# Strassen's scheme in one decoder layer: thirteen early weight sums built by adding transfers in DRAM instead of on VectorE

## Chip, cores, metric

One core of one Trainium2 chip runs the whole kernel in one launch. The metric is the device time in microseconds (us); lower is better. Names of the engines: TensorE (PE) multiplies matrices, VectorE (DVE) and ScalarE (ACT) work element by element, GpSimd (POOL) does little work of its own here and issues transfers on a software queue (q0 in the profile), SyncE (SP) issues the weight loads on a hardware queue (q1). All transfers are moved by the same 16 DMA engines.

## The reference, cut to what matters

One layer of a decoder trunk over 256 tokens of width 2048, all in float32:

```python
a = rmsnorm(h, attn_norm)
proj = a @ w_in                        # 2048 x 5184: MLA q, latent, rope key, MoBA q, k, v
kv = rmsnorm(c_kv, kv_norm) @ w_ukv    # 512 x 2048
...
h = h + concat(out_mla, out_moba) @ w_o            # 2048 x 2048
f = rmsnorm(h, ffn_norm)
h = h + (silu(f @ w_gate) * (f @ w_up)) @ w_down   # 2048 x 5632, twice, and back
g = sigmoid(rmsnorm(h, ple_norm) @ w_ple_gate)     # 2048 x 2048
h = h + g * (p @ w_ple_proj)
return rmsnorm(h, final_norm)
```

## The kernel before, in words

**Products in three parts.** Every float32 operand is split into a high part (rounded to float32r) and a low part (the rest), and a product is three matmuls that accumulate in one bank of PSUM: high x high, low x high, high x low (`three`, L385 to L390). For a weight tile, ACT makes the high part by a cast (`split_hi`, L337), and DVE the low part by a subtraction (`split_lo`, L348). The parts go into a ring of 12 places of 512 columns (`ringh`, `ringl`), later also into `more` and `most`.

**Units and groups.** The work is a list of units; a unit is a pair of 128-row tiles of a weight matrix with up to 1024 columns, 1 MB, loaded by SP (`load`, L220) into one of three buffers (`raw`; five from the MLP on). A group is all units of one output: ga, q0, u0, q1, u1, qk0, qk1, v (the attention's projections), wo0 and wo1 (its output), then g0, g1 and so on for gate and u0, u1 and so on for up of the MLP, d for down, and pg, pe at the end. The columns of q1 (512) and the two halves of qk0 and qk1 (512 each) are loaded in rows of 2 KB, most others in rows of 4 KB. A buffer is free again when both splits of its unit are done. The load of unit i+3 stands in the program at unit i; SP issues it as soon as the buffer is free. Inside ACT and DVE all work is in the order of the program, and attention, norms and the emptying of banks are woven in between the splits by a list of tasks (`add`, `step`).

**The start.** x arrives already turned; ACT and DVE split it (`x_parts`) and form the sum of its squares. When ga's last product is done, ACT takes the square root that x's norm needs (L157), DVE finishes the norm's factor, and ACT empties ga's banks (L860) so that q0's products may start.

**Strassen's scheme.** In the MLP (from its second group on; the MLP's up groups carry the names u0 to u4 as well) most units use the scheme with seven products instead of eight: for a weight block with quarters b11, b12, b21, b22, the products use b11, b22, b21 and four sums of quarters t1 to t4 on the weights' side, and four sums S1 to S4 of quarters of the activations (made in `act_transpose` at L140 to L143, and in `sums_of`). `seven` issues the seven products and, at a group's end, combines them (L465 to L469). The weight sums of an ordinary unit are made by DVE in place in its buffer (L347, L350, L351).

**Early sums.** For 13 of these units (`EARLY`: three of g1, two each of u1, u2, u3, u4, one each of g2 and g3) the sums are made long before, while attention runs. The task `early_sums` (L356 to L376) does it unit by unit: POOL loads the block from DRAM into the SBUF tile `wsums` (L366), the task waits until PE has been given a certain number of columns, DVE makes the sums by three subtractions (L372 to L374), and POOL stores the four sums, 128 x 2048, into a DRAM tile (L376). When the unit's turn comes in the MLP, SP loads b11, b21, b22 from the weights (L209, L210) and the four sums from that tile (L211). The tiles `wsums` stand in SBUF places that later hold other things (`f0l`, `more_sums`). The task starts at unit 5 of ga, on two units first, and with the rest at unit 8; a copy of one element on POOL (L364) makes the first transfer wait for the load that is three units ahead.

**Adding transfers.** POOL can issue a transfer that adds to its target. Before the change the kernel does so in the MLP: `gate_add` (`stage<-U`, L1018), `add_later` (`hd<-copied`, L937, its target in DRAM) and `split_hi` of some units of down (`morel<-raw`, L336). POOL issues in the order of the program; an instruction that waits holds up all behind it.

Of the kernel before, what the change touches and what calls it, by code (L numbers as in the profile page):

```python
# [8 lines left out]
F32 = mybir.dt.float32  # L9
# [4 lines left out]
ALU = mybir.AluOpType  # L14
# [21 lines left out]
def kernel(ctx, tc, x, w_in, w_ukv, w_o, w_gate, w_up, w_down, w_ple_gate, w_ple_proj,  # L36
                             final_norm, x_turned, p_turned, columns_in, out):
    nc = tc.nc
# [73 lines left out]
    def act_transpose(src, k0, g0, dst, kd0=None, scaled=False, sums=None):  # L112

        kd0 = k0 if kd0 is None else kd0
        part = src[:, :, k0 * 128:k0 * 128 + 256]
        if scaled:
            part = S["nrm"][:, (k0 // 2) % 2]
        b = obank()  # L120
        for i in range(2):
            for t in range(NT):
                nc.tensor.transpose(b[:, (2 * i + t) * 128:(2 * i + t + 1) * 128],  # L123
                                    part[:, t, i * 128:(i + 1) * 128], ident)
        if sums is None:
            both = [(dst[0][:, kd0 + i, :], dst[1][:, kd0 + i, :], b[:, i * 256:(i + 1) * 256],
                     gain[:, g0 + k0 + i:g0 + k0 + i + 1]) for i in range(2)]
            for hi, _, ps, g in both:
                nc.scalar.mul(hi, ps, g)
            for hi, lo, ps, g in both:  # L130
                nc.vector.scalar_tensor_tensor(lo, ps, g, hi.bitcast(F32), op0=ALU.mult, op1=ALU.subtract)
            return
        whole, some = S["nrm"][:, 2], S["nrm"][:, 3]
        for i in range(2):
            nc.scalar.mul(whole[:, i], b[:, i * 256:(i + 1) * 256], gain[:, g0 + k0 + i:g0 + k0 + i + 1])
        split_psum(dst[0][:, kd0:kd0 + 2, :], dst[1][:, kd0:kd0 + 2, :], whole)
        a11, a21, a12, a22 = (whole[:, i, t * 128:(t + 1) * 128] for i in range(2) for t in range(2))
        four = some.rearrange("q a (b c) -> q (a b) c", b=2)
        tt = nc.vector.tensor_tensor
        tt(four[:, 0], a21, a22, op=ALU.add)  # L140
        tt(four[:, 2], a21, a11, op=ALU.subtract)
        tt(four[:, 1], four[:, 0], a11, op=ALU.subtract)
        tt(four[:, 3], a12, four[:, 1], op=ALU.subtract)  # L143
        split_psum(sums[0], sums[1], four)

    def square_sum(src, acc):
# [192 lines left out]
    def split_lo(jb, c0=0, c1=None, n=1, row=slice(None)):  # L339

        if units[jb.unit].adding:
            return
        h, l, r = (x[:, row] for x in by_row_tile(n, *parts_of(jb), raw_of(jb)))
        tt = nc.vector.tensor_tensor
        f = quarters(jb) if jb.kind == "21" and not units[jb.unit].early else None
        if f is not None:
            tt(f[:, 0:2], f[:, 1:2].to_broadcast([128, 2, 512]), f[:, 0:4:3], op=ALU.subtract)  # L347
        tt(l[:, :, c0:c1], r[:, :, c0:c1], h[:, :, c0:c1].bitcast(F32), op=ALU.subtract)  # L348
        if f is not None:
            tt(f[:, 3], f[:, 3], f[:, 0], op=ALU.subtract)  # L350
            tt(f[:, 2], f[:, 2], f[:, 3], op=ALU.subtract)  # L351

    todo_early = []

    def early_sums(tag, enough, wait, landed=None):

        made = 0
        while todo_early and made < enough:
            u = todo_early.pop(0)
            made += 1  # L360
            f = big.tile([128, 4, 512], F32, name="wsums", tag=tag)
            (w, c0, _), k0 = u.srcs[0], u.ks[0] * 128
            if landed is not None:
                nc.gpsimd.tensor_copy(f[:, 0, 0:1], landed)  # L364
                landed = None
            nc.gpsimd.dma_start(f.rearrange("q (k a) c -> q k (a c)", k=2),  # L366
                                w[k0:k0 + 256, c0:c0 + 1024].rearrange("(k q) c -> q k c", q=128))
            since = columns[0]
            while columns[0] < since + wait() or S["crowded"]:
                yield 1  # L370
            tt = nc.vector.tensor_tensor
            tt(f[:, 0:2], f[:, 1:2].to_broadcast([128, 2, 512]), f[:, 0:4:3], op=ALU.subtract)  # L372
            tt(f[:, 3], f[:, 3], f[:, 0], op=ALU.subtract)
            tt(f[:, 2], f[:, 2], f[:, 3], op=ALU.subtract)  # L374
            u.early = dram.tile([128, 2048], F32, name=f"wsums{u.name}{u.idx}")
            nc.gpsimd.dma_start(u.early, f.rearrange("q a c -> q (a c)"))  # L376

    def split(jb):
        if not jb.cast:
# [62 lines left out]
    def seven(u, turn):  # L442
# [18 lines left out]
        if turn == 3 and u.sevens_end:  # L461
            U = S["U"] = big.tile([128, NT, 1024], F32, name="U", tag="vb")
            c1, c2 = U[:, :, 0:512], U[:, :, 512:1024]
            tt = nc.vector.tensor_tensor
            nc.scalar.copy(c1[:, 0], st["m1"])  # L465
            tt(c2[:, 0], c1[:, 0], st["m6"], op=ALU.add)
            tt(c1[:, 1], c2[:, 0], st["m7"], op=ALU.add)
            tt(c2[:, 0], c2[:, 0], st["m5"], op=ALU.add)
            tt(c2[:, 1], c1[:, 1], st["m5"], op=ALU.add)  # L469
            B["rot"], B["next"] = st["free"], 0  # L470
            if u.into is not None:
                def join(hs=S["h"][:, :, u.into:u.into + 1024]):
                    tt(hs, hs, U, op=ALU.add)
                    yield 1
                add(join())

    def sums_of(parts, k0, pairs, at, tag="vb"):

        for n, kk in enumerate(pairs):
            both = big.tile([128, 2, 2, SEQ], F32, name="both", tag=tag)  # L480
            whole, some = both[:, 0], both[:, 1]
            h, l = (x[:, kk - k0:kk - k0 + 2] for x in parts)
            tt = nc.vector.tensor_tensor
            tt(whole, h.bitcast(F32), l.bitcast(F32), op=ALU.add)
            a11, a21, a12, a22 = (whole[:, i, t * 128:(t + 1) * 128] for i in range(2) for t in range(2))
            hi, lo = (aT[i][:, at + 2 * n:at + 2 * n + 2] for i in range(2))
            four = some.rearrange("q a (b c) -> q (a b) c", b=2)
            tt(four[:, 0], a21, a22, op=ALU.add)
            tt(four[:, 1], four[:, 0], a11, op=ALU.subtract)
            tt(four[:, 2], a21, a11, op=ALU.subtract)  # L490
            tt(four[:, 3], a12, four[:, 1], op=ALU.subtract)
            split_psum(hi, lo, some)
            yield 1

# [834 lines left out]
    for i, u in enumerate(units):  # L1329
# [5 lines left out]
        S["long"] = u.name in ("ga", "q0", "u0", "wo0", "wo1")  # L1335
        S["crowded"] = u.name == "v" and u.idx > 0 or u.name == "wo0" and u.idx < 4
        if u.name == "ga" and u.idx == 5:
            todo_early.extend(x for x in units if x.early)
            add(early_sums("f0l", 2, lambda: 53248, raw[i + 3][:, 0, 0:1]))
        if u.name == "ga" and u.idx == 8:  # L1340
            add(early_sums("more_sums", 99, lambda: 57344 if S["long"] else 34816))
        if u.name == "g1" and u.idx == 0:
            S["mid"] = S.pop("turned")
        if u.name == "wo0":
# [87 lines left out]
```

## Time and profile before

| what | value |
|---|---|
| median of 3 runs | 1180.9 us (1180.17 to 1181.25) |
| the profiled execution | 1180.28 us, of which the span of the program is 1178.5 us |
| idle share of PE by the page | 1% |
| matmuls | 5477 |
| bytes moved by DMA | 287.80 MB, mean 244 GB/s |
| loads of wsums by POOL | 13 of 1 MB, issued from 31.7 to 326.2 us |
| stores of wsums by POOL | 13 of 1 MB, issued from 57.7 to 343.7 us |

In the page's slices (40 of 29.5 us), PE is full in all but the last, and the granted PE clock is at nine tenths or more throughout. The DMA row is highest at the start:

```profile
PE   9999999999999999999999999999999999999996
PEld 7888888899888888888888888888888888888886
DVE  6866756776557689999999899989998989897474
ACT  6745746456456756667566666757575756465453
DMA  9896787755683776686959596868868795846531
```

Each digit is the busy share of a slice in tenths. DVE is at 5 to 8 tenths over attention (the first 14 slices) and near full in the MLP.

### The profile page before, as it was taken

What the parts mean: (1) busy time and instruction counts of PE and PEld (TensorE: products, weight loads), DVE (VectorE), ACT (ScalarE), POOL (GpSimd) and SP (SyncE); (2) the same over time, 40 slices, a digit from 0 to 9 for tenths busy, and PEclk for the clock granted to TensorE, in tenths of its full rate; (3) what the DMA queues carried; (4) which work ended last, traced back from release to release, by engine and by line L of the source; (5) the groups of instructions that cost most, each with busy time, mean ns of one, the idle gap of its engine ahead of it and who ended that gap; (6) DMA issues with size and microseconds to landing.
All of it is one profiled execution on the core that took longest, in us unless ns stands there. A gap on an engine that the chain in (4) does not pass through costs nothing.

```text
span 1178.5 us, 14590 instructions
## 1 busy us (share of the span) xinstructions
PE 1167.4 (99%) x5477; PEld 978.3 (83%) x5477; DVE 952.9 (81%) x1127; ACT 710.7 (60%) x898; POOL 50.2 (4%) x73
## 2 busy tenths in 40 slices
PE   9999999999999999999999999999999999999996
PEld 7888888899888888888888888888888888888886
DVE  6866756776557689999999899989998989897474
ACT  6745746456456756667566666757575756465453
POOL 5000000000000000000000000000000000000000
PEclk9999999999999999999999999999999999999999
DMA  9896787755683776686959596868868795846531
GB/s 328 298 337 202 288 299 258 267 185 206 220 330 130 280 260 220 235 283 208 353 171 334 154 348 210 291 214 321 240 214 255 283 276 195 326 153 218 201 107 72
DMA packets 85880, 287.80 MB, mean 244 GB/s; under 512 B 5681, under 2 KB 7985, under 8 KB 81201
## 3 DMA queue, kind: packets, MB, share of 16 engines
q1 hardware_dynamic: 76352, 239.71, 56.7%
q0 software_dynamic: 8880, 46.14, 14.2%
q10 hardware_dynamic: 576, 1.02, 0.3%
q8 instruction: 43, 0.70, 0.2%
q14 instruction: 29, 0.23, 0.1%
HBM read 252.24 MB, written 26.21 MB: 236 GB/s over the span
## 4 chain that ended last, share of the span: by engine, by line
PE 95%; DMA 2%; ACT 1%; DVE 1%; SPq 0%; issue 0%; ACTq 0%; DVEq 0%
PE bank L390 30%; PE bank L388 30%; PE bank L389 30%; DMA raw<-in_w_in 2%; PE bank L591 1%; PE bank L1052 1%; PE bank L123 1%; PE bank L620 1%; ACT ringh L337 1%; PE bank L614 0%; PE bank L594 0%; PE bank L726 0%; DMA xT<-in_x_turned 0%; PE bank L621 0%; ACT aT L109 0%
## 5 line engine op out<-in xcount | busy, mean ns | idle before, releaser
L337 ACT CAST ringh<-raw 128x1024 fp32r<-128x1024 f32 (+5 forms) x310 | 372.7, 1239 | 274.9 <-PE bank L389 112.0
L348 DVE TENSOR_TENSOR ringl<-raw,ringh 128x1024 fp32r<-128x1024 f32 (+5 forms) x310 | 444.7, 1457 | 101.9 <-ACT ringh L337 100.0
L388 PE MATMUL bank<-ringh,aT 128*128 128x512 f32 (+3 forms) x713 | 274.7, 385 | 0.2
L390 PE MATMUL bank<-ringl,aT 128*128 128x512 f32 (+3 forms) x713 | 270.8, 380 | 0.0
L389 PE MATMUL bank<-ringh,aT 128*128 128x512 f32 (+3 forms) x713 | 270.3, 379 | 0.0
L390 PEld LDWEIGHTS bank<-ringl,aT 128*128 128x128 f32 x713 | 134.1, 188 | 25.3 <-DVE ringl L348 0.9
L388 PEld LDWEIGHTS bank<-ringh,aT 128*128 128x128 f32 x713 | 134.2, 188 | 24.7 <-ACT ringh L337 1.0
L389 PEld LDWEIGHTS bank<-ringh,aT 128*128 128x128 f32 x713 | 134.3, 188 | 23.8 <-DVE aT L658 0.2
L337 ACT CAST moreh<-raw 128x1024 fp32r<-128x1024 f32 (+2 forms) x70 | 79.8, 1173 | 19.9 <-DVE raw L347 9.2
L348 DVE TENSOR_TENSOR morel<-raw,moreh 128x1024 fp32r<-128x1024 f32 (+2 forms) x66 | 85.5, 1317 | 1.8 <-ACT moreh L337 1.3
L388 PE MATMUL bank<-ringh,ffTh 128*128 128x512 f32 x204 | 79.5, 390 | 0.0
L337 ACT CAST most<-raw 128x1024 fp32r<-128x1024 f32 (+2 forms) x58 | 56.8, 1005 | 37.5 <-DVE raw L347 14.4
L390 PE MATMUL bank<-ringl,ffTh 128*128 128x512 f32 x204 | 79.4, 389 | 0.0
L389 PE MATMUL bank<-ringh,ffTl 128*128 128x512 f32 x204 | 79.4, 389 | 0.0
L348 DVE TENSOR_TENSOR most<-raw,most 128x1024 fp32r<-128x1024 f32 (+2 forms) x58 | 66.3, 1164 | 1.6 <-ACT most L337 1.5
L347 DVE TENSOR_TENSOR raw<-raw 128x1024 f32<-128x1024 f32 x51 | 62.5, 1225 | 1.7
L389 PEld LDWEIGHTS bank<-ringh,ffTl 128*128 128x128 f32 x204 | 38.3, 188 | 8.0
L388 PEld LDWEIGHTS bank<-ringh,ffTh 128*128 128x128 f32 x204 | 38.3, 188 | 7.9
L390 PEld LDWEIGHTS bank<-ringl,ffTh 128*128 128x128 f32 x204 | 38.3, 188 | 7.9
L351 DVE TENSOR_TENSOR raw<-raw 128x512 f32<-128x512 f32 x51 | 35.3, 692 | 1.8
L350 DVE TENSOR_TENSOR raw<-raw 128x512 f32<-128x512 f32 x51 | 34.9, 684 | 0.0
L388 PE MATMUL bank<-most,aT 128*128 128x512 f32 x88 | 34.6, 394 | 0.0
(356 smaller groups left out, 1958.6 us busy)
## 6 DMA issues: line engine op xcount, KB each, us to landing
raw<-in_w_down SPq DMA_DIRECT2D x44, 1024.0 KB, 7.2
raw<-in_w_gate SPq DMA_DIRECT2D x35, 1024.0 KB, 7.4
raw<-in_w_up SPq DMA_DIRECT2D x32, 1024.0 KB, 7.5
raw<-in_w_in SPq DMA_DIRECT2D x40, 512.0 KB, 5.4
raw<-in_w_o SPq DMA_DIRECT2D x16, 1024.0 KB, 5.6
raw<-in_w_ple_gate SPq DMA_DIRECT2D x16, 1024.0 KB, 5.0
raw<-in_w_in SPq DMA_DIRECT2D x8, 1024.0 KB, 5.0
wsums<-in_w_up POOLq DMA_DIRECT2D x8, 1024.0 KB, 7.1
```

The source lines that it names most:

```text
L123: nc.tensor.transpose(b[:, (2 * i + t) * 128:(2 * i + t + 1) * 128], part[:, t, i * 128:(i + 1) * 128], ident)
L337: nc.scalar.copy(h[:, :, c0:c1], r[:, :, c0:c1])
L347: tt(f[:, 0:2], f[:, 1:2].to_broadcast([128, 2, 512]), f[:, 0:4:3], op=ALU.subtract)
L348: tt(l[:, :, c0:c1], r[:, :, c0:c1], h[:, :, c0:c1].bitcast(F32), op=ALU.subtract)
L350: tt(f[:, 3], f[:, 3], f[:, 0], op=ALU.subtract)
L351: tt(f[:, 2], f[:, 2], f[:, 3], op=ALU.subtract)
L388: nc.tensor.matmul(b, xh, h, start=start, stop=False)
L389: nc.tensor.matmul(b, xl, h, start=False, stop=False)
L390: nc.tensor.matmul(b, xh, l, start=False, stop=stop)
L591: nc.tensor.matmul(s[:, c0:c0 + nk], qT[:, q * 128:(q + 1) * 128], kT[:, 0:nk], start=True, stop=qpe is None)
L620: nc.tensor.matmul(o[:, 0:256], v(0), pT[:, 0:256], start=True, stop=False)
L1052: nc.tensor.transpose(b[:, (2 * i + t) * 128:(2 * i + t + 1) * 128], st[:, t, (k + i) * 128:(k + i + 1) * 128], ident)
```

## The change

The early sums no longer pass through SBUF and DVE. For each of the 13 units, POOL copies quarters of the weight block straight into the unit's DRAM tile and then lets transfers add to it, in four rounds: b11 into the first and the fourth place, b22 into the second, b21 into the third; then b12 is added to the first and second; then the second is added to the fourth; then the fourth to the third. Two units are taken together, round by round. All of these transfers are issued at unit 5 of ga, as one list on POOL, with no waiting for columns; what orders them is only their dependence on each other. A transfer of a round waits for the landing of those of the round before.

So that additions suffice, the signs of the scheme are turned: t1 to t4 of the ordinary units and S1 to S4 are formed with other signs and operands, in the same number of instructions of the same shapes, and two combinations at a group's end become `m5 - c2` and `m5 - c1`.

```diff
         tt = nc.vector.tensor_tensor
-        tt(four[:, 0], a21, a22, op=ALU.add)
-        tt(four[:, 2], a21, a11, op=ALU.subtract)
+        tt(four[:, 0], a21, a22, op=ALU.subtract)
+        tt(four[:, 2], a11, a21, op=ALU.subtract)
         tt(four[:, 1], four[:, 0], a11, op=ALU.subtract)
-        tt(four[:, 3], a12, four[:, 1], op=ALU.subtract)
+        tt(four[:, 3], four[:, 1], a12, op=ALU.add)
...
         if f is not None:
-            tt(f[:, 0:2], f[:, 1:2].to_broadcast([128, 2, 512]), f[:, 0:4:3], op=ALU.subtract)
+            tt(f[:, 0:2], f[:, 1:2].to_broadcast([128, 2, 512]), f[:, 0:4:3], op=ALU.add)
...
-            tt(f[:, 3], f[:, 3], f[:, 0], op=ALU.subtract)
-            tt(f[:, 2], f[:, 2], f[:, 3], op=ALU.subtract)
+            tt(f[:, 3], f[:, 3], f[:, 0], op=ALU.add)
+            tt(f[:, 2], f[:, 2], f[:, 3], op=ALU.add)
...
-    def early_sums(tag, enough, wait, landed=None):
...
-            f = big.tile([128, 4, 512], F32, name="wsums", tag=tag)
...
-            nc.gpsimd.dma_start(f.rearrange("q (k a) c -> q k (a c)", k=2),
-                                w[k0:k0 + 256, c0:c0 + 1024].rearrange("(k q) c -> q k c", q=128))
-            since = columns[0]
-            while columns[0] < since + wait() or S["crowded"]:
-                yield 1
-            tt = nc.vector.tensor_tensor
-            tt(f[:, 0:2], f[:, 1:2].to_broadcast([128, 2, 512]), f[:, 0:4:3], op=ALU.subtract)
-            tt(f[:, 3], f[:, 3], f[:, 0], op=ALU.subtract)
-            tt(f[:, 2], f[:, 2], f[:, 3], op=ALU.subtract)
-            u.early = dram.tile([128, 2048], F32, name=f"wsums{u.name}{u.idx}")
-            nc.gpsimd.dma_start(u.early, f.rearrange("q a c -> q (a c)"))
+    def early_sums(them, landed):
+
+        nc.gpsimd.tensor_copy(const.tile([128, 1], F32, name="landed"), landed)
+
+        def sums_of_one(u):
+            u.early = dram.tile([128, 2048], F32, name=f"wsums{u.name}{u.idx}")
+            e = u.early.rearrange("q (a c) -> q a c", a=4)
             (w, c0, _), k0 = u.srcs[0], u.ks[0] * 128
+            b11, b12, b21, b22 = (w[k0 + 128 * k:k0 + 128 * k + 128, c0 + c:c0 + c + 512].rearrange(
+                "q (a c) -> q a c", a=1) for k in range(2) for c in (0, 512))
+            nc.gpsimd.dma_start(e[:, 0:4:3], b11.to_broadcast([128, 2, 512]))
+            nc.gpsimd.dma_start(e[:, 1:2], b22)
+            nc.gpsimd.dma_start(e[:, 2:3], b21)
+            yield
+            nc.gpsimd.dma_start(e[:, 0:2], b12.to_broadcast([128, 2, 512]), accum_op=ALU.add)
+            yield
+            nc.gpsimd.dma_start(e[:, 3:4], e[:, 1:2], accum_op=ALU.add)
+            yield
+            nc.gpsimd.dma_start(e[:, 2:3], e[:, 3:4], accum_op=ALU.add)
+
+        for n in range(0, len(them), 2):
+            both = [sums_of_one(u) for u in them[n:n + 2]]
+            while both:
+                both = [g for g in both if next(g, g) is None]
...
-            tt(c2[:, 0], c2[:, 0], st["m5"], op=ALU.add)
-            tt(c2[:, 1], c1[:, 1], st["m5"], op=ALU.add)
+            tt(c2[:, 0], st["m5"], c2[:, 0], op=ALU.subtract)
+            tt(c2[:, 1], st["m5"], c1[:, 1], op=ALU.subtract)
...
         if u.name == "ga" and u.idx == 5:
-            todo_early.extend(x for x in units if x.early)
-            add(early_sums("f0l", 2, lambda: 53248, raw[i + 3][:, 0, 0:1]))
-        if u.name == "ga" and u.idx == 8:
-            add(early_sums("more_sums", 99, lambda: 57344 if S["long"] else 34816))
+            early_sums([x for x in units if x.early], raw[i + 3][:, 0, 0:1])
```

On POOL, behind the rotary tables in ga, this stood before the change (out<-in, a load of `wsums` is L366, a store L376):

```order
L364 COPY wsums<-raw_114 128x1
L366 DMA wsums<-in_w_gate 128x2x1024 x2
L376 DMA wsumsg_535<-wsums 128x2048
L366 DMA wsums<-in_w_gate 128x2x1024
L376 DMA wsumsg_654<-wsums 128x2048
L366 DMA wsums<-in_w_up 128x2x1024
```

And this stands there now; `wsumsg_326` and `wsumsg_330` are the DRAM tiles of the first two units, L363 to L365 the copies, L367, L369 and L371 the three rounds of adding:

```order
L363 DMA wsumsg_326<-in_w_gate 128x2x512
L364 DMA wsumsg_326<-in_w_gate 128x512
L365 DMA wsumsg_326<-in_w_gate 128x512
L363 DMA wsumsg_330<-in_w_gate 128x2x512
L364 DMA wsumsg_330<-in_w_gate 128x512
L365 DMA wsumsg_330<-in_w_gate 128x512
L367 DMA wsumsg_326<-in_w_gate 128x2x512
L367 DMA wsumsg_330<-in_w_gate 128x2x512
L369 DMA wsumsg_326<-wsumsg_326 128x512
L369 DMA wsumsg_330<-wsumsg_330 128x512
L371 DMA wsumsg_326<-wsumsg_326 128x512
L371 DMA wsumsg_330<-wsumsg_330 128x512
```

A load and a store per unit have become six transfers, 26 transfers 78, and every one stands on POOL ahead of the MLP's first adding transfer. On DVE, in group q1, where the low parts of its units are split off, the three subtractions of an early unit stood between two splits before the change:

```order
L574 TENSOR_TENSOR qpT<-qpT,ra 128x4x32
L348 TENSOR_TENSOR ringl<-raw_113,ringh 128x1024
L372 TENSOR_TENSOR wsums<-wsums 128x1024
L373 TENSOR_TENSOR wsums<-wsums 128x512
L374 TENSOR_TENSOR wsums<-wsums 128x512
L348 TENSOR_TENSOR ringl<-raw_114,ringh 128x1024
L348 TENSOR_TENSOR ringl<-raw_112,ringh 128x1024
```

and now the splits follow one another:

```order
L574 TENSOR_TENSOR qpT<-qpT,ra 128x4x32
L348 TENSOR_TENSOR ringl<-raw_113,ringh 128x1024
L348 TENSOR_TENSOR ringl<-raw_114,ringh 128x1024
L348 TENSOR_TENSOR ringl<-raw_112,ringh 128x1024
```

The same happens at 13 places; PE, ACT and SP keep their instructions and their order.

More of the change, by code (lines that the diff above doesn't have):

```diff
@@ L346, in split_lo @@
         if f is not None:
-            tt(f[:, 0:2], f[:, 1:2].to_broadcast([128, 2, 512]), f[:, 0:4:3], op=ALU.subtract)
+            tt(f[:, 0:2], f[:, 1:2].to_broadcast([128, 2, 512]), f[:, 0:4:3], op=ALU.add)
         tt(l[:, :, c0:c1], r[:, :, c0:c1], h[:, :, c0:c1].bitcast(F32), op=ALU.subtract)
         if f is not None:
-            tt(f[:, 3], f[:, 3], f[:, 0], op=ALU.subtract)
-            tt(f[:, 2], f[:, 2], f[:, 3], op=ALU.subtract)
-    todo_early = []
-    def early_sums(tag, enough, wait, landed=None):
[L357 to L360, printed above, removed]
-            f = big.tile([128, 4, 512], F32, name="wsums", tag=tag)
-            (w, c0, _), k0 = u.srcs[0], u.ks[0] * 128
[L363 to L366, printed above, removed]
-                                w[k0:k0 + 256, c0:c0 + 1024].rearrange("(k q) c -> q k c", q=128))
-            since = columns[0]
-            while columns[0] < since + wait() or S["crowded"]:
-                yield 1
-            tt = nc.vector.tensor_tensor
-            tt(f[:, 0:2], f[:, 1:2].to_broadcast([128, 2, 512]), f[:, 0:4:3], op=ALU.subtract)
-            tt(f[:, 3], f[:, 3], f[:, 0], op=ALU.subtract)
-            tt(f[:, 2], f[:, 2], f[:, 3], op=ALU.subtract)
-            u.early = dram.tile([128, 2048], F32, name=f"wsums{u.name}{u.idx}")
-            nc.gpsimd.dma_start(u.early, f.rearrange("q a c -> q (a c)"))
@@ L487, in sums_of @@
             four = some.rearrange("q a (b c) -> q (a b) c", b=2)
-            tt(four[:, 0], a21, a22, op=ALU.add)
+            tt(four[:, 0], a21, a22, op=ALU.subtract)
             tt(four[:, 1], four[:, 0], a11, op=ALU.subtract)
-            tt(four[:, 2], a21, a11, op=ALU.subtract)
-            tt(four[:, 3], a12, four[:, 1], op=ALU.subtract)
+            tt(four[:, 2], a11, a21, op=ALU.subtract)
+            tt(four[:, 3], four[:, 1], a12, op=ALU.add)
             split_psum(hi, lo, some)
```

## The prediction, made before the result was known

> **What bounds the kernel now.** I read the page first (busy time, chain), then the table of windows, then the chain stretch by stretch where the windows left something open.
>
> ```profile
> span 1178.5 us, 14590 instructions
> ...
> PE 1167.4 (99%) x5477; PEld 978.3 (83%) x5477; DVE 952.9 (81%) x1127; ACT 710.7 (60%) x898; POOL 50.2 (4%) x73
> ...
> PE 95%; DMA 2%; ACT 1%; DVE 1%; SPq 0%; issue 0%; ACTq 0%; DVEq 0%
> ```
>
> Between first and last instruction lie 1178.5 us, and 95% of the chain that ended last is TensorE (PE). A busy PE need not be a PE at its best, so I look for places where it waits:
>
> ```profile
> core 0: us, PE busy (x) PEld busy (x) DVE busy (x) ACT busy (x) POOL busy (x), PEclk, DMA share, GB/s
> 48.76:150.00 101.24, 101.24 (x521) 86.46 (x522) 70.03 (x107) 60.68 (x91) 6.19 (x10) 1.00 0.78 276
> 150.00:260.00 110.00, 110.00 (x546) 93.80 (x545) 74.44 (x106) 52.60 (x80) 7.04 (x11) 1.00 0.72 256
> 260.00:430.00 170.00, 170.00 (x845) 145.09 (x844) 112.72 (x154) 107.38 (x168) 1.81 (x3) 1.00 0.66 237
> 430.00:1167.00 737.00, 737.00 (x3347) 612.76 (x3346) 655.00 (x691) 452.32 (x512) 16.34 (x17) 1.00 0.71 237
> sum 1118.24, PE 1118.24 PEld 938.10 DVE 912.20 ACT 672.99 POOL 31.38; mean PE 279.56 PEld 234.53 DVE 228.05 ACT 168.25 POOL 7.85
> ```
>
> From 48.76 us to 1167 us PE is busy in 1118.24 of 1118.24 us at a granted clock of 1.00. There its own instruction stream is the limit; the change leaves that stream alone. VectorE (DVE) is busy 70.03 of 101.24 us and 74.44 of 110.00 us: it has air there, and nobody on the chain waits for it. What is left is the start before 48.76 us, where transfers and ScalarE (ACT) set the pace, and the last 11 us behind the last matmul, which the change does not touch. At the end of the start the chain runs so:
>
> ```profile
> 36.71 6.69 DMA raw<-in_w_in
> 43.51 1.92 ACT ringh L337
> 45.44 1.28 ACT L157
> 48.02 0.70 ACT stage L860
> 48.76 0.50 PE bank L388
> 49.26 0.23 PE bank L389
> ```
>
> The load issued at 36.71 us lands 6.69 us later; ACT, in order, casts it (L337), only then does the square root of x's norm, then empties the first group's bank (L860), and with that q0's first matmul starts at 48.76 us. The PE rows just ahead:
>
> ```profile
> 48.26 0.37 PE L390 MATMUL bank<-ringl,aT 128*128 128x448 f32 x1
> 48.76 0.50 PE L388 MATMUL bank<-ringh,aT 128*128 128x512 f32 x1
> ```
>
> PE was itself busy until 48.26 + 0.37 = 48.63 us, so it waits 0.13 us there. That is all the idle time that an earlier release could give back at any place the change reaches.
>
> **The change, part by part.** *VectorE.* Thirteen triples (L372 to L374) go:
>
> ```profile
> L372 DVE TENSOR_TENSOR wsums<-wsums x13: 1206/1218/1226, 54.7 to 340.7; 128x1024 f32<-128x1024 f32 x13
> L373 DVE TENSOR_TENSOR wsums<-wsums x13: 691/692/695, 55.9 to 341.9; 128x512 f32<-128x512 f32 x13
> L374 DVE TENSOR_TENSOR wsums<-wsums x13: 691/692/694, 56.7 to 342.7; 128x512 f32<-128x512 f32 x13
> ```
>
> 13 x (1.218 + 0.692 + 0.692) = 33.8 us less for DVE, all between 54.7 and 343 us, where PE never waits. Worth on the path: 0 (bounds 0 and the 0.13 us above). It only makes the splits behind them earlier, and so frees load buffers earlier.
>
> *Signs.* Subtractions become additions or swap operands, with the same counts and shapes. A subtraction of 128x1024 (L347) has a mean of 1225 ns, an addition of 128x1024 (L677) took 1.23 us:
>
> ```profile
> L347 DVE TENSOR_TENSOR raw<-raw 128x1024 f32<-128x1024 f32 x51 | 62.5, 1225 | 1.7
> 33.34 1.23 DVE L677 TENSOR_TENSOR squares<-squares 128x1024 f32<-128x1024 f32 x1 [0.46 <-ACT squares L675]
> ```
>
> Cost 0. Two of them now take the PSUM operand first; no row shows that order, and I take 0 with 0 to 0.1 us each as bounds, off the path either way.
>
> *Transfers, in engine time.* Before, each of the 13 units is read once and stored once, 2 x 1 MB. Afterwards it is copied within DRAM (b11 twice, b22, b21: 1 MB) and gets 1 MB of additions (512 + 256 + 256 KB). The trace has the price of both kinds: from 35 to 39 us plain transfers alone ran, from 512 to 516 us one adding transfer (stage<-U) alone.
>
> ```profile
> 35.00:39.00 4.00, 4.00 (x20) 3.55 (x19) 3.93 (x7) 3.30 (x5) 0.00 (x0) 1.00 1.03 413
> 512.00:516.00 4.00, 4.00 (x20) 3.30 (x19) 4.00 (x3) 1.00 (x2) 0.00 (x0) 1.00 1.09 203
> 638.00:641.00 3.00, 3.00 (x15) 2.50 (x14) 2.96 (x5) 1.18 (x2) 0.00 (x0) 1.00 1.05 257
> ```
>
> 413 GB/s plain, 203 GB/s adding: a plain MB takes 2.54 us, an added MB 5.17 us. So 13 x 2 x 2.54 = 66 us become 13 x (2.54 + 5.17) = 100 us, 34 us more, and all of it may start at once rather than be spread by column counts. That the rows are 2 KB long, and source and target both in DRAM, no row shows; by these rows I bound the added MB between 2.5 us (plain rate) and 10 us (twice the adding rate) and take 5.17. What they meet:
>
> ```profile
> q1 hardware_dynamic: 21461, 56.25, 50.6%
> q0 software_dynamic: 5408, 27.26, 22.6%
> ```
>
> From 30 to 350 us SP's queue (q1, the weights) took 50.6% of the engines and POOL's (q0) 22.6%, 72 us. With 34 us more: (162 + 106) of 320 us, 84%. It fits as a whole, yet as POOL's list runs as fast as it can, the engines will be near full until it ends.
>
> *When the list ends.* A pair of units has four rounds, each waiting for landings of the round before (the rows of POOL's order).
>
> ```profile
> hd<-copied POOLq DMA_DIRECT2D x8, 1024.0 KB, 8.2
> wsums<-in_w_gate POOLq DMA_DIRECT2D x5, 1024.0 KB, 7.2
> ```
>
> 7.2 us for the copies and at most 8.2 us for each adding round give 32 us a pair, seven pairs 224 us: from 31.7 us until some 256 us; by engine time alone 31.7 + 100 = 132 us. Behind the waiting adds on POOL stand only later pairs and an adding transfer of the MLP (L1018). That one and the first reader of a sum (L211) are issued at:
>
> ```profile
> L211 SPq DMA_DIRECT2D raw<-wsumsg x5: 326/327/330, 452.9 to 721.5; - x5
> 510.44 0.90 POOL L1018 DMA_DIRECT2D stage<-U  x1 [166.22 <-DVE U L469]
> ```
>
> So these waits hold up nobody: 0. Even a list of five times the engine time would have the three sums of g1, which come first in it, by 31.7 + 3 x 5 x 7.7 = 147 us.
>
> *The first collision.*
>
> ```profile
> 31.73 1.73 POOL L366 DMA_DIRECT2D wsums<-in_w_gate  x2 [0.32 <-POOL wsums L364]
> raw<-in_w_in SPq DMA_DIRECT2D x1, 1024.0 KB, 4.8
> ```
>
> POOL starts at 31.73 us as before, with 2 MB as before, but at 37 to 38 us, when the first unit's copies have landed, an adding transfer of 512 KB joins (512 KB at 203 GB/s: 2.6 us). The load of 36.71 us, which the chain above needs, took 6.69 us beside the old 2 MB; the next one, issued between 41.5 and 42 us with POOL silent, took 4.8 (second row). Bounds: -1.9 us (no collision, of which PE can use 0.13) and +2.6 us (the adding transfer goes wholly ahead). The nearest case is the same 2 MB, so about 0, plus a part of the add: I take **+0.4 us**.
>
> *Steady contention, 49 to 256 us.* A load may come late by as much as its buffer allows. The tightest place I found is in group q1, where three casts wait for their loads:
>
> ```profile
> 108.26 4.73 SPq L220 DMA_DIRECT2D raw<-in_w_in  x3
> 113.58 1.05 ACT L337 CAST ringh<-raw 128x1024 fp32r<-128x1024 f32 x1 [2.24 <-DMA raw<-in_w_in]
> 120.91 0.58 PE L388 MATMUL bank<-ringh,aT 128*128 128x512 f32 x1
> ```
>
> The load of 108.26 us is cast at 113.58 us and first used by PE at 120.91 us (found by counting matmuls), 12.65 us from issue to use. Cast 1.05 and split 1.22 us leave 10.4 us for the landing, which took 5.3. Loads beside an adding transfer, three at once, took this long in the MLP:
>
> ```profile
> raw<-in_w_up SPq DMA_DIRECT2D x3, 1024.0 KB, 10.7
> ```
>
> (those issued from 511 to 517 us), while PE stayed busy. So 0 by the nearest rows; the bounds are 0 and the 34 us of extra engine time, should every microsecond of it end as a late load.
>
> The Trainium skill, "DMA: Bandwidth & Descriptors", section "Queues, rings and completion order", says that an engine drains a whole packet of one queue, typically 9 to 17 descriptors, before it turns to the next. By that rule a load could stand behind a whole 512 KB add at each turn, and the +2.6 us would hold at the first collision. The row of 638 to 641 us, 257 GB/s with both kinds under way, does not tell the two apart, since a mix by turns of either size gives it.
>
> Sum: 0 + 0 + 0.4 + 0 = **+0.4 us**. On the profiled execution of 1180.28 us (span 1178.5 and 1.8 around it) that is 1180.7; the median of the three runs is 0.6 higher, 1180.9, so I forecast **1181.3 us**.
>
> **The rivals.** (1) *Loads starve in the stretch with three buffers* (slower). Place: groups q1, qk0 and qk1, whose loads have rows of 2 KB. If an engine takes one row of each queue in turn, a load's row (2 KB at 413 GB/s on 16 engines, 79 ns) stands against an adding row (161 ns) and gets a third. A unit of 24 matmuls at 0.23 us (a step of PE in the chain) lasts 5.5 us and needs 2.54 us of load, 46%. At a third the loads fall short by 13% of the time. Adding takes 67 us of engine time, about 100 us at two thirds; half of that may meet these groups: 50 x 0.13 = 6.5 us, about 1187.5. It decides once a landing exceeds 10.4 us again and again. Against: between rounds POOL's queue is empty for a landing's latency, and freed DVE time issues loads earlier. For: q0 and q1 both near full, and casts that already wait 2.24 us.
> (2) *The first collision in full*: the load waits out the whole 512 KB add, +2.6 us, 1183.5. For: the load of 36.71 us landed 1.9 us later than the one after it, so it did stand behind POOL's transfers. Against: the copies now have short rows, which may give way sooner. The rule of the Trainium skill above would bring about this case.
> (3) *Faster*: the 33.8 us of DVE show up. Against: 1118.24 of 1118.24. At most 0.13 us, 1180.8, unless the records hide a wait within busy PE.
> (4) *The change doesn't do what it says*: the adding list runs so slowly that PE waits for the sums at g1. That takes over 421 us (31.7 to 452.9) for three units that have 23 us of engine time; no row speaks for it.
>
> **How the numbers follow.** Forecast 0.71; (1) 0.16; (2) 0.09; (3) 0.03; (4) 0.01. A measurement of this kernel tells about 0.2% (2.4 us) from no change. (1), (2) and (4) are slower: 0.26; (3) faster: 0.03. The range goes from 1180.0, just below the lowest repeat of 1180.17, up to 1187, which takes in (2) and the smaller half of (1); the larger half (0.08), (4) and what could fall below (0.06) leave out about 0.15.
>
> **What would show it.** Right: DVE's busy time about 34 us lower, POOL's queue with about 100 us of engine time and silent from some 130 to 256 us on, PE again without idle time behind its q0 start, and that start between 48.6 and 51 us. Wrong: PE rows in groups q1 to v with idle time before them that ends with ringh or ringl, casts that wait several microseconds for raw, or sums that land after 452 us.

## The result and the profile after

The changed kernel is slower: a median of 1190.1 us over four runs (1188.04 to 1193.29) beside 1180.5 us (1180.12 to 1181.25) for the kernel before, a ratio of 1.0083 with a 95% interval of 1.0058 to 1.0107. That is above the range that was forecast. The profiled execution took 1188.04 us, 7.8 us more than the profiled one of before; its span is 7.5 us longer. Those 7.5 us can be located.

First the page of the changed kernel: the span, the busy times, the chain by engine, POOL's queue over the whole span, and a group of loads with their median time to landing.

```profile
span 1186.0 us, 14620 instructions
...
PE 1168.8 (99%) x5477; PEld 978.8 (83%) x5477; DVE 920.8 (78%) x1088; ACT 710.4 (60%) x898; POOL 94.1 (8%) x125
...
q0 software_dynamic: 14704, 46.14, 18.7%
...
PE 92%; DMA 4%; ACT 1%; DVE 1%; issue 0%; SPq 0%; ACTq 0%; DVEq 0%
...
raw<-in_w_in SPq DMA_DIRECT2D x40, 512.0 KB, 10.6
```

The last two rows in the page of before:

```profile
q0 software_dynamic: 8880, 46.14, 14.2%
...
raw<-in_w_in SPq DMA_DIRECT2D x40, 512.0 KB, 5.4
```

DVE lost the forecast work (952.9 to 920.8 us). POOL's queue moves the same 46.14 MB, but takes 18.7% of 1186.0 us instead of 14.2% of 1178.5: 222 us instead of 167, so 54 us more, where the prediction had 34. These loads of w_in take twice as long to land, and transfers have doubled their share of the chain.

Next the list of PE's waits in the changed kernel (engine and line that waited, what it waited for, us in total, times, longest):

```profile
PE bank L388 <- ACT stage L883: 3.5, 1, 3.5
PE bank L388 <- ACT stage L860: 2.8, 1, 2.8
```

The only other one, of 2.0 us, belongs to the start and stood there before. These two are new, and both name ACT emptying a bank, not a weight that is late. Four rows of PE's timeline place them: first of before, the second unit of q0 and the first product of u1, then the same two of after with the first product of q0 ahead of them.

```profile
54.34 0.39 PE L388 MATMUL bank<-ringh,aT 128*128 128x512 f32 x1
133.58 0.36 PE L388 MATMUL bank<-ckvT,ringh 128*128 128x256 f32 x1
```

```profile
51.12 0.79 PE L388 MATMUL bank<-ringh,aT 128*128 128x512 f32 x1 [2.75 <-ACT stage L860]
...
58.20 0.39 PE L388 MATMUL bank<-ringh,aT 128*128 128x512 f32 x1
...
141.22 0.39 PE L388 MATMUL bank<-ckvT,ringh 128*128 128x256 f32 x1 [3.48 <-ACT stage L883]
```

q0 starts 2.36 us late (51.12 for 48.76). Its first unit then takes 7.08 us rather than 5.58, so that the second starts 3.86 us late. At u1 the delay is 7.64 us, and it stays there to the end. The windows of the changed kernel, cut at these places:

```profile
core 0: us, PE busy (x) PEld busy (x) DVE busy (x) ACT busy (x) POOL busy (x), PEclk, DMA share, GB/s
48.36:50.87 2.51, 0.01 (x1) 0.00 (x0) 1.40 (x6) 1.42 (x3) 0.00 (x0) 1.00 1.08 304
50.87:54.28 3.41, 3.16 (x8) 2.48 (x9) 3.20 (x11) 3.41 (x7) 0.85 (x1) 0.50 1.08 267
...
100.00:140.00 40.00, 37.73 (x196) 31.92 (x194) 17.88 (x24) 20.36 (x35) 12.71 (x18) 1.00 1.02 277
140.00:260.00 120.00, 118.78 (x597) 101.05 (x598) 64.77 (x95) 61.70 (x94) 27.99 (x36) 1.00 1.02 273
```

The extra 1.5 us of q0's first unit are the second row: for 3.41 us after the wait PE was granted half its clock. And from 100 to 260 us the DMA engines are full (1.02, where before they stood at 0.72 to 0.78), yet outside the wait at u1 (137.74 to 141.22 us) PE works through. Saturated transfers as such cost it nothing there.

How the late loads reach PE is seen twice. The chain of waits of the changed kernel at q0's start (start, us, what):

```profile
35.39 10.39 DMA raw<-in_w_in
45.88 1.91 ACT ringh L337
47.81 1.28 ACT L157
50.38 0.70 ACT stage L860
51.12 0.79 PE bank L388
```

It is the chain of before, link by link, but the load lands after 10.39 us instead of 6.69. It was issued 1.3 us earlier, so 2.4 us are left. What it met is told by POOL's timeline of the changed kernel, the first of the first two units' copies, the first transfer of the first adding round, and the last of the whole list:

```profile
30.02 0.94 POOL L363 DMA_DIRECT2D wsumsg<-in_w_gate  x1
...
40.10 1.24 POOL L367 DMA_DIRECT2D wsumsg<-in_w_gate  x1 [6.28 <-DMA wsumsg<-in_w_gate]
...
271.28 0.81 POOL L371 DMA_DIRECT2D wsumsu<-wsumsu  x1 [5.56 <-DVE ringl L348]
```

The load of 35.39 us met the copies; the first add was only issued at 40.10, and its first rows ran at 43.9 us. In the trace's records of single rows the 2 MB of copies took 7.1 us of all engines' time, where the 2 MB of loads of before took 5.2 (a mean of 218 against 163 ns for a row of 4 KB; the medians are alike, 160 and 159, so some of the rows carry the difference). The load's own first row ran at 39.74 us, when three quarters of the copies were through.

At u1, ACT's timeline of the changed kernel (start, us, what, and in brackets the idle time before it and what ended it):

```profile
136.47 1.90 ACT L337 CAST ringh<-raw 128x2048 fp32r<-128x2048 f32 x1 [1.89 <-DMA raw<-in_w_ukv]
...
140.48 1.27 ACT L883 ACTIVATE stage<-bank,rx 128x512 f32<-128x512 f32 x2
```

The cast of 136.47 us makes the high part of u1's *second* unit, which PE needs only some 12 us later. But behind it on ACT, in the order of the program, stand a piece of the softmax and the emptying of q1's bank (L883), and that bank u1's *first* product needs at once. Before, this cast found its load landed:

```profile
128.02 1.90 ACT L337 CAST ringh<-raw 128x2048 fp32r<-128x2048 f32 x1
```

It did so only just: the load, issued at 119.64 us, took 8.3 us, until 127.94. In the changed kernel the chain ahead of the cast runs so:

```profile
115.25 8.04 DMA raw<-in_w_in
123.37 1.05 ACT ringh L337
124.45 1.24 DVE ringl L348
125.70 10.69 DMA raw<-in_w_ukv
```

A load of q1 lands late, its cast and split come late, so its buffer is free late and the next load is issued late, and then that one lands late as well. The cast starts 8.45 us later than before. PE is 3.9 us late by then; of the other 4.5, some 2.1 come from the late issue and 2.4 from the longer landing. About 0.8 us were to spare behind the cast (before, L883 began 4.56 us after the cast, now 4.01, and PE then started 0.3 us behind the emptied bank, now at once), and 3.7 reach PE.

The groups of ACT's waits from 48 to 300 us say how common waits for loads have become; first before, then after:

```profile
ACT ringh L337 <- DMA raw<-in_w_in: 4.2, 3, 2.2
...
ACT ringh L337 <- DMA raw<-in_w_o: 1.7, 1, 1.7
```

```profile
ACT ringh L337 <- DMA raw<-in_w_in: 37.2, 11, 6.2
...
ACT ringh L337 <- DMA raw<-in_w_ukv: 6.6, 3, 4.2
```

Nearly 44 us in 14 waits, where before there were 5.9 us in 4. PE felt one of the 14 in this stretch (the cast behind which q0's start waits lies ahead of it).

### The profile page after: what moved, and what is told of

It is laid out like the page before. It is cut to its first block, busy times and chain, and to the rows that moved or that the text cites. A ratio compares the mean times of both kernels' runs of the same rounds, so it can differ in the third digit from the quotient of the medians.

```text
span 1186.0 us, 14620 instructions
## 1 busy us (share of the span) xinstructions
PE 1168.8 (99%) x5477; PEld 978.8 (83%) x5477; DVE 920.8 (78%) x1088; ACT 710.4 (60%) x898; POOL 94.1 (8%) x125
## 3 DMA queue, kind: packets, MB, share of 16 engines
q0 software_dynamic: 14704, 46.14, 18.7%
q10 hardware_dynamic: 576, 1.02, 0.3%
## 4 chain that ended last, share of the span: by engine, by line
PE 92%; DMA 4%; ACT 1%; DVE 1%; issue 0%; SPq 0%; ACTq 0%; DVEq 0%
PE bank L388 29%; PE bank L390 29%; PE bank L389 29%; DMA raw<-in_w_in 3%; DMA raw<-in_w_ukv 1%; PE bank L1052 1%; ACT ringh L337 1%; PE bank L123 1%; PE bank L591 1%; DVE ringl L348 1%; PE bank L620 1%; DMA xT<-in_x_turned 0%; PE bank L614 0%; PE bank L726 0%; PE bank L621 0%
## 5 line engine op out<-in xcount | busy, mean ns | idle before, releaser
L390 PE MATMUL bank<-ringl,aT 128*128 128x512 f32 (+3 forms) x713 | 271.3, 381 | 0.0
## 6 DMA issues: line engine op xcount, KB each, us to landing
raw<-in_w_in SPq DMA_DIRECT2D x40, 512.0 KB, 10.6
wsumsu<-in_w_up POOLq DMA_DIRECT2D x16, 512.0 KB, 10.4
```

Source lines behind the costliest of these rows:

```text
L390: nc.tensor.matmul(b, xh, l, start=False, stop=stop)
```

## The experiments

The first theory was: the list of transfers fills the engines; a cast that waits for its load holds up what stands behind it on ACT; this hurts at two places. Rivals were the turned signs, the price of adding, and that any place would be hit.

**Signs alone.** The new signs everywhere, early sums made on DVE as before.

```diff
-    def early_sums(them, landed):
+    def early_sums(tag, enough, wait, landed=None):
...
+            tt(f[:, 0:2], f[:, 1:2].to_broadcast([128, 2, 512]), f[:, 0:4:3], op=ALU.add)
+            tt(f[:, 3], f[:, 3], f[:, 0], op=ALU.add)
+            tt(f[:, 2], f[:, 2], f[:, 3], op=ALU.add)
```

> The changed kernel, with the thirteen early sums made on VectorE through SBUF again (with additions, the new signs kept). Theory: the loss comes from the list of transfers within DRAM alone; this gives 1180.5 us, within 0.5, and q0's first matmul at 48.8 us. Rival, that the turned signs or PSUM operands cost something: it stays above 1182 us.

1180.7 us, ratio 1.0001 (0.9991 to 1.0010). The signs cost nothing; the whole loss is the list's. In this run's profile q0 starts at 49.33 us, behind a wait of 1.1 us, and not at 48.8: the load before it, issued at 35.75 us beside plain loads, took 8.23 us. By so much the start can vary without the list.

**The list at another time.** It starts at q0's third unit, or at the first of qk0.

```diff
-        if u.name == "ga" and u.idx == 5:
+        if u.name == "q0" and u.idx == 2:
```

> The changed kernel, with the same list of transfers issued from unit 2 of q0 on (some 25 us later) instead of unit 5 of ga. Theory: 3.9 us of the loss are the first collision (the load before q0, and the slow PE clock behind the gap), and they vanish; the wait at u1's first product stays or moves: 1183 to 1186 us. Rival, that any start of the list costs the same at the place it meets: 1188 us or more.

```diff
-        if u.name == "ga" and u.idx == 5:
+        if u.name == "qk0" and u.idx == 0:
```

> The changed kernel with the list issued at the first unit of qk0 (near 150 us). Theory: the places that cannot bear late loads are q0's start and the stretch of q1 and u1, where loads are short of time; behind it PE has 6 to 10 us to spare at each unit, so the waits sum to less than 2 us: 1181 to 1183 us. Rival, that every stretch with three buffers pays: 1186 us or more.

The first took 1189.9 us, 1.0080 (1.0065 to 1.0095), no better than the change; the second 1194.7 us, 1.0123 (1.0106 to 1.0140), worse. PE's two largest waits with the list from q0, then the two largest with the list from qk0, both beside the start's:

```profile
PE bank L388 <- ACT stage L883: 5.2, 1, 5.2
...
PE bank L620 <- DVE att L597: 1.0, 1, 1.0
```

```profile
PE bank L123 <- ACT stage L971: 3.6, 1, 3.6
PE bank L388 <- DVE h L918: 2.6, 1, 2.6
```

In the first, q0's start is clean, but u1's wait has grown from 3.5 to 5.2 us. In the second both old waits are gone, and between 275 and 370 us there are new ones: beside these two, smaller waits for the softmax (1.5 and 1.4 us) and one of 0.9 us for a low part (`ringl`). The wait for L918 shows the same mechanism with DVE in it: ACT's cast of 336.61 us waits 6.77 us for a load of w_o, DVE's split of 338.56 us waits for that cast, and behind the split stands L918, for which PE waits until 341.59 us. "Only two places are sensitive" fell: at each of the three starts that were tried, work on ACT or DVE that PE waits for stood behind a late load.

**ACT's order at the two places.** At q0's start the square root is issued ahead of the cast; at u1 the casts of later units go behind the emptying.

```diff
+            if i == 8:
+                step()
             if i >= 5:
                 high_parts(todo + late if weave or "mid" in S and units[i + 1].early else todo)
...
-            if n % 2 == 0:
+            if n % 2 == 0 and i != 8:
                 step()
```

> The changed kernel, with ScalarE's square root for x's norm put ahead of the cast of q0's second unit at the end of ga; transfers unchanged. Theory: PE lost time at q0's start only because ScalarE, in order, held the norm behind a cast that waited for a late load. Then the cast of 45.9 to 47.8 us is followed at once by the emptying of the bank, q0 starts at 48.5 us, the clock keeps its full value there, and the total is 3.9 us lower than the changed kernel: about 1185.5 us. Rival, that the load itself is needed that early: q0 starts at 51 us as before, 1189 us.

```diff
-                    not may_wait(i, jobs[nxt]):
+                    not may_wait(i, jobs[nxt]) and not (u.name == "q1" and u.last and jobs[nxt].unit > i + 1):
```

> The changed kernel, with the cast of u1's second unit put behind the emptying of q1's banks; transfers unchanged. Theory: the 3.5 us that PE waits at u1's first product are a bank that ScalarE empties only behind a cast that waits for its load; the wait there falls below 0.5 us and the total by about 3 us, to 1186.5 us. Rival, that the late weights themselves stop PE: the wait only moves to u1's second unit, 1189 us.

With the root ahead: 1188.1 us, 1.0059 (1.0043 to 1.0076). PE's waits beside the start's:

```profile
PE bank L388 <- ACT stage L883: 4.2, 1, 4.2
...
PE bank L614 <- ACT att L610: 1.2, 1, 1.2
```

L860 is gone from the list: q0 starts at 48.28 us although its load is as late as in the change. So ACT's order is what passed the lateness on there. Of the 3.9 us that this removed little is gained: u1 waits 0.7 us longer, attention 1.2 us, and from 135.55 us on PE's clock is halved for 6.8 us. The medians differ by 2.0 us, but the intervals overlap, and the profiled executions differ by 0.1 us. With the emptying ahead: 1191.7 us, 1.0096 (1.0073 to 1.0118). q0's wait is still there (3.0 us). Of u1's wait 0.96 us is left, and ACT's timeline shows where the rest went:

```profile
147.69 1.90 ACT L337 CAST ringh<-raw 128x2048 fp32r<-128x2048 f32 x1 [4.90 <-DMA raw<-in_w_in]
...
151.08 0.45 ACT L615 COPY att<-bank 128x384 f32<-128x384 f32 x1
```

The next cast waits 4.90 us for its load, the softmax behind it is late, and PE's product of attention waits 4.89 us for L615. Both runs show the mechanism, and that mending one place moves the wait to the next.

**The list without adding, thinner, or paced.** First the same transfers as plain copies (the sums then hold copies of quarters); then one unit at a time instead of two; then one unit at a time where every round also waits until PE has been given 10000 more columns.

```diff
-            nc.gpsimd.dma_start(e[:, 0:2], b12.to_broadcast([128, 2, 512]), accum_op=ALU.add)
+            nc.gpsimd.dma_start(e[:, 0:2], b12.to_broadcast([128, 2, 512]))
...
-            nc.gpsimd.dma_start(e[:, 3:4], e[:, 1:2], accum_op=ALU.add)
+            nc.gpsimd.dma_start(e[:, 3:4], e[:, 1:2])
...
-            nc.gpsimd.dma_start(e[:, 2:3], e[:, 3:4], accum_op=ALU.add)
+            nc.gpsimd.dma_start(e[:, 2:3], e[:, 3:4])
```

> The changed kernel with the adding of the three later rounds left out: the same transfers, waits and bytes, but plain copies, so the early sums hold copies of quarters instead of sums. Theory: copies alone are enough for the first collision (the load before q0 stands behind 2 MB of them), so q0 still starts near 51 us; the rounds behind weigh half as much, the loads land near 7 us instead of 10, and the wait at u1's first product falls below 1 us: about 1184.5 us. Rival, that the price of adding makes no difference because the list refills the queue anyway: 1188 to 1190 us.

```diff
-        for n in range(0, len(them), 2):
-            both = [sums_of_one(u) for u in them[n:n + 2]]
+        for n in range(0, len(them)):
+            both = [sums_of_one(u) for u in them[n:n + 1]]
```

> The changed kernel with the units of the list taken one by one instead of two by two: the same transfers, but half as many in flight. Theory: what hurts is how much of the list stands in the engines' queues ahead of a load; with 1 MB of copies instead of 2 at the start the load before q0 lands near 43.5 us and q0 starts below 49.5 us, loads land near 7 to 8 us, the wait at u1 is below 1 us, the list ends 60 to 100 us later: 1181 to 1183 us. Rival, that the share of the engines over the whole list counts: it stays at 1187 us or more.

```diff
-        for n in range(0, len(them), 2):
-            both = [sums_of_one(u) for u in them[n:n + 2]]
+        mark, seen = (const.tile([128, 52], F32, name=x) for x in ("mark", "seen"))
+        k = 0
+        for n in range(0, len(them)):
+            both = [sums_of_one(u) for u in them[n:n + 1]]
             while both:
                 both = [g for g in both if next(g, g) is None]
+                since = columns[0]
+                while columns[0] < since + 10000:
+                    yield 1
+                nc.vector.memset(mark[:, k:k + 1], 0.0)
+                nc.gpsimd.tensor_copy(seen[:, k:k + 1], mark[:, k:k + 1])
+                k += 1
...
-            early_sums([x for x in units if x.early], raw[i + 3][:, 0, 0:1])
+            add(early_sums([x for x in units if x.early], raw[i + 3][:, 0, 0:1]))
```

> The changed kernel, three buffers, units one by one, and ahead of every round POOL waits for a mark that VectorE sets at least 10000 columns of PE behind the last one, so that the list spreads evenly until about 390 us. Theory: what the change dropped with the column counts is the spreading; with gaps between rounds a load meets at most one round and lands within 8 us, q0 starts below 49.2 us, the wait at u1 is below 1 us: 1180.5 to 1182 us. Rival, that one round beside the loads of q1 and u1 is already too much with three buffers: 1185 us or more.

| kernel | us | ratio (95%) | last transfer of the list issued at | landing of 512 KB of w_in | PE's two largest waits behind the start |
|---|---|---|---|---|---|
| the change | 1190.1 | 1.0083 (1.0058 to 1.0107) | 271.3 us | 10.6 us | 3.5, 2.8 us |
| without adding | 1192.0 | 1.0099 (1.0084 to 1.0114) | 216.7 us | 7.7 us | 5.0, 3.3 us |
| one unit at a time | 1186.0 | 1.0051 (1.0036 to 1.0066) | 367.3 us | 6.2 us | 2.8 us alone |
| paced rounds | 1183.4 | 1.0026 (1.0014 to 1.0037) | 377.8 us | 6.7 us | 2.2, 0.9 us |

Without adding, the transfers are cheaper (POOL's queue falls from 222 to 185 us of engine time), and it helps nothing, against the forecast of 1184.5 us: the list waits only for its own landings, so it runs through faster and fills the engines nearly as well while it lasts (0.91 to 0.99 of them from 60 to 200 us, in the change 0.98 to 1.04). The price of adding isn't the cause. Nor is it the sum of ACT's waits: there ACT waits only 24.5 us for loads from 48 to 300 us, and PE loses as much. Fewer transfers under way at once do help: all four executions with one unit at a time are faster than the fastest of the change (1184.55 to 1187.92 beside 1188.04 us). With one unit there is no wait at q0's start, where only 1 MB of copies stands before the load, and u1's wait is smaller; pacing takes more of that away, but the list is stretched and there is a wait of 2.2 us at 287.8 us, where the kernel before has none. PE's two largest waits with paced rounds:

```profile
PE bank L628 <- DVE att L605: 2.2, 1, 2.2
...
PE bank L396 <- ACT stage L891: 0.9, 1, 0.9
```

Both last two runs came out between the two theories' numbers.

**A fourth load buffer.** If the lateness of the loads is what matters, and not the engines' load, then loads that are asked for earlier may be as slow as they like. The place in SBUF that the old early sums used is free now; it becomes a fourth buffer from q0's first unit until wo0. The list is as in the change; in the second kernel it goes one unit at a time.

```diff
+    fourth = big.tile([128, 2048], F32, name="fourth", tag="more_sums")
...
-        r = raws[u.raw][:, 0:nk * n].rearrange("q (k c) -> q k c", k=nk)
+        r = (fourth if u.raw == 9 else raws[u.raw])[:, 0:nk * n].rearrange("q (k c) -> q k c", k=nk)
...
+            if i == 9:
+                order.insert(0, 9)
+            if u.name in ("wo0", "wo1") and order[0] == 9:
+                order.pop(0)
```

> The changed kernel with a fourth load buffer from q0 to v, in the SBUF place that the change set free; list as in the change. Theory: the engines have room for list and loads together, only the loads are not asked for early enough; with one more load ahead the load before q0 is issued near 30 us, ahead of the list, the casts no longer wait for loads, and the waits of PE vanish: 1180.5 to 1182 us. Rival, that the loads get too small a share of the engines while the list runs: the casts wait all the same, and the wait at u1 stays over 2 us: 1185 us or more.

> The fourth buffer and the units of the list one by one, together. Theory: the loads are asked for early enough and less of the list stands ahead of them, so no cast waits over 2 us, PE has no wait over 0.2 us behind q0's start, and the time is that of the kernel before within its spread: 1180.3 to 1180.9 us; not below, since PE is then busy without a gap as it was before. Rival, that the list costs PE something else than waits on late loads (a slower clock, transfers of instructions): it stays at 1181.5 us or more.

The first took 1181.5 us (1179.54 to 1185.59, 10 runs), 1.0011 (1.0002 to 1.0020): nearly all of the loss is gone. PE's waits in it behind the start's, the landing of its loads, and ACT's waits for loads from 48 to 300 us:

```profile
PE bank L625 <- DVE att L602: 0.5, 1, 0.5
PE bank L619 <- ACT att L615: 0.3, 1, 0.3
```

```profile
raw<-in_w_in SPq DMA_DIRECT2D x30, 512.0 KB, 13.3
```

```profile
ACT ringh L342 <- DMA raw<-in_w_o: 5.1, 2, 4.3
ACT ringh L342 <- DMA fourth<-in_w_in: 4.7, 2, 4.5
...
ACT ringh L342 <- DMA raw<-in_w_ukv: 1.1, 1, 1.1
ACT ringh L342 <- DMA raw<-in_w_in: 0.3, 1, 0.3
```

This is the run that decides. The list is untouched, its last transfer is issued at 265.6 us, POOL's queue takes 18.8%, and the loads land even later than in the change (13.3 us for 10.6). But ACT waits 11.2 us for them instead of 44, PE's two waits are gone, and from 60 to 260 us PE is busy in 200.00 of 200.00 us with the engines at 0.96 to 1.05. So neither the engines' load nor the landing time cost anything by themselves; what cost was a landing time longer than three buffers look ahead, with ACT's queue in between. About 1 us of loss is left in the median; the two small waits sum to 0.8 us.

The second took 1182.7 us (1179.76 to 1184.58, 11 runs), 1.0016 (1.0007 to 1.0025), a miss of about 2 us by the expectation of at most 1180.9, and, as the intervals overlap, neither clearly better nor worse than the first. Two casts still wait 3.8 and 3.4 us for their loads, where none was to wait over 2 us. Its profiled execution was its fastest, 1179.76 us, without any wait behind q0's start; what the slower ones spent isn't seen. Neither version beats the kernel before.

## Why the prediction was wrong

By its own steps:

- *VectorE*, worth 0: right. DVE has 32.1 us less to do (33.8 forecast), and no run gained from it.
- *Signs*, 0: right, shown by the first experiment.
- *Transfers, in engine time*, +34 us: too small. 54 us were measured. By the records of single rows the adds took 87 us for the 67 of the forecast, the copies 40 for 33, and the loads and stores that they replace had taken 72 rather than 66. It mattered less than it looks: the run without adding took 37 us of that back and lost as much.
- *When the list ends*, by 256 us, holds up nobody: its last transfer was issued at 271.3 us, and no wait for a sum appeared. Right in effect.
- *The first collision*, +0.4 us, bounds -1.9 and +2.6: mis-sized. 2.36 us were measured, near the upper bound, with another partner. The step held "the same 2 MB" to be equal, and looked for the extra in the adding transfer. The 2 MB of copies were the dearer part; the add ran only beside the load's last 1.9 us, and without any adding q0 still waits 3.3 us. That also takes the ground from the second rival as it was priced (the load behind the whole add). A part may be chance: the start was 0.6 us late in the run with the new signs alone, too. The Trainium skill, "DMA: Bandwidth & Descriptors", section "Queues, rings and completion order", which stood behind that rival, is neither borne out nor refuted: the load did wait for the copies queued ahead, but the records don't tell packets of 9 to 17 descriptors from another share. And 1.5 us came on top that no step had: PE's half clock behind the wait. The start at 51.12 us lies just outside the 48.6 to 51 us that the prediction named for being right.
- *Steady contention*, 0: **this is the step that failed**, as the prediction put it: "leave 10.4 us for the landing, which took 5.3", and from there "So 0 by the nearest rows". It asked whether the weights arrive before PE multiplies with them. They do: in the changed kernel no wait of PE names ringh or ringl, and the load of q1 that takes 8.04 us is in time for that. It didn't ask what else stands behind the cast on ACT. A cast stands on ACT long before PE needs its result, and while it waits for its load it holds up the emptying of a bank that PE needs at once. The air to count was that from issue to *cast*, and from there to whatever PE needs next from ACT, not from issue to product. In the row that the prediction quotes the first of these is used up: the cast already waits 2.24 us for its load. At u1's second unit, where the prediction didn't look, the load of before had 0.1 us to spare, and what stands behind the cast some 0.8 us. Nor did it count that a late load frees its buffer late, so that lateness is handed on to the load behind it. At u1 this cost 3.7 us.
- *Rival (1)*, loads starve, 1187.5 us: it had the cause (landings above 10 us, ACT's casts waiting), but expected PE to be short of weights all through the groups. What came was one wait at one place in this stretch. Its threshold, landings above 10.4 us, doesn't hold: PE lost as much with 7.7 us (without adding) and next to nothing with 13.3 us (fourth buffer). Its price is too small by its own premises, too: at a third of the engines a unit takes 2.54 / 0.33 = 7.7 us instead of 5.5, which in 50 us costs about 14 us and not 6.5.
- What would show it wrong: casts that wait several microseconds for raw were rightly named as a sign. Waits ended by ringh or ringl were not what came.

The three other runs of the change, 1189.2 to 1193.3 us, have no profile. Their mean granted clock is 0.992 to 0.995 beside 0.996 of the profiled one, and 0.004 of 1190 us is 4.8 us, about what the slowest of them is longer. That speaks for further stretches of half clock, but it is argued, not shown. Open, too: why copies within DRAM and adds are dearer than the rows that the prediction took for them, and the 1 to 2 us that the last kernels with four buffers lose in some runs.

## What to carry to other kernels

To judge a slower transfer, take the instruction that waits for it and read what stands behind that instruction on its in-order engine; air up to the use of the data proves nothing. Moving or mending the place that shows moves the wait, as long as a background list runs as fast as its own landings allow: look further ahead with another buffer, or pace the list. Here one engine was busy all along, so the work taken off another gained nothing, and dearer transfers could only lose.

## What was not expected of the hardware

A short wait of PE can cost again in clock. From windows like those above and the records of the granted clock behind them:

| kernel | wait of PE | stretch with granted clock 0.50 |
|---|---|---|
| the change, q0 | 2.8 us | 3.4 us from 50.87 |
| the change, u1 | 3.5 us | none |
| list from q0, u1 | 5.2 us | 6.8 us from 136.85 |
| one unit at a time, u1 | 2.8 us | 3.4 us from 137.69 |
| root ahead, attention and u1 | 1.2 and 4.2 us | 6.8 us from 135.55 |
| emptying ahead, q0 | 3.0 us | 6.8 us from 50.73 |
| emptying ahead, attention | 4.9 us | 6.8 us from 149.72 |
| list from qk0, until 341.59 us | 2.6 us | none |
| list from qk0, until 369.42 us | 3.6 us | 6.8 us from 368.17 |
| paced rounds, attention | 2.2 us | none |

The lengths, 3.4 and 6.8 us, are one and two times the idle window that the Trainium skill gives in "TensorE: Matmul & The Clock Gate", section "Part 1: The HAM clock gate (the "warmup" mystery)": about 3.4 us, running freely. That one wait of 2.8 us halved the clock and one of 3.5 us did not fits such windows, by an estimate: counted on from 50.87 us in steps of 3.41 us, one ends at 139.6 us, in the middle of u1's wait, and leaves some 1.9 and 1.6 us of it on either side, while 2.5 us of q0's wait (48.36 to 50.87 us) lie in one window. The other runs fit too, with one exception. Each is cut into windows of 3.41 us, counted from a fall of its own clock; of the nine full-clock windows behind which the clock fell, eight hold 2.0 us or more without a matmul, and those behind which it stayed full hold at most 1.9 us. The ninth (root ahead, from 132.14 us) holds 1.7 us, so how idle time is counted stays open. Where the Trainium skill asks for at least one idle window, the measurement decides: 2.0 us of idle time in one were enough (one unit at a time, 134.27 to 136.31 us).

And two queues don't share from the first moment: a load that came while 2 MB of copies were queued on the other queue ran its first row 4.3 us after its issue (35.39 to 39.74 us). Beside the 2 MB of loads of before it was 2.6 us (36.71 to 39.30), with the other queue still empty 1.0 us (30.03 to 31.05).
